# Rotation tables by doubling on ScalarE and VectorE, weight stores one half later, norm transposes later

## The chip, the cores and the metric

The kernel runs on one core of a Trainium2 chip. The metric is the device time of one execution in microseconds (us), and the time of the kernel before is the median of three runs. A core has five engines, each with a queue of its own that it works through in order: TensorE (PE, matmuls and transposes, results in PSUM), VectorE (DVE), ScalarE (ACT), GpSimd (POOL) and SyncE (SP, which here only issues DMAs). ACT and POOL issue DMAs too. Engines wait for one another by semaphores; a wait stands in the queue, and what is behind it waits as well.

## What is computed

One layer of a decoder trunk on x of 2048 x 1024 float32, with 256 memory tokens:

```python
h = rmsnorm(x, mix_norm_w);  proj = h @ w_in                       # 2816 + 12 columns
y_s5  = s5_mixer(proj[..., :256], ...)                             # 16 groups of a diagonal SSM, 64 complex states each
y_ssd = ssd_mixer(z, xbc, dt, ...)                                 # conv, chunks of 128, 12 heads
x = x + concat([y_s5, y_ssd]) @ w_out
x = x + cross_attention(rmsnorm(x), rmsnorm(mem), wq, wk, wv, wo)
x = x + conv_ffn(rmsnorm(x), w_up, conv_w, conv_b, w_down)
return rmsnorm(x, final_norm_w)
```

The part that the change touches most is the S5 group. Its recurrence over blocks of 8 steps is done as a real scan of magnitudes after a rotation, and for that each of the 16 groups needs a table of cos and sin, powers j = 0 to 255 of one unit complex number per state: 128 partitions x 2 x 256 values.

## The kernel before

The program is written with generators, and a framework turns it into one instruction order per engine, with semaphores where data or buffers demand them. The order on each engine follows the order of the text, with priorities and the framework's own forecast of what is ready when.

*Mixer (first 730 us).* `MixerIn.run` goes through four blocks of 512 rows (b = 0 to 3). Each block makes 22 projections (`proj`, n = 0 to 21): 24 matmuls of 128x512 each, since every float32 product is split into a high and a low fp32r part and done as three matmuls (`mm3`, L127 to L129). After each half projection `k.step()` advances three lists of generators by one `yield`: `fg` (the chunk scan `ssd` of the half block before), `bg` (`norm1_rest`, and `ssq` once per block) and `xg` (`s5_setup`, from the second half of block 0 on). So "one step later" means half a projection later.

*Weights.* `fetch` runs three projections ahead. A weight that is new is loaded into two staging tiles (tag `r`, L115), split on ACT (L102) and DVE (L103) into four tiles (tag `w`), and at one of the passes the split parts are stored to DRAM (`wSd`, L319); later blocks load the parts straight into `w` tiles (L317). `store` says at which block n is stored; up to and including that block it is loaded and split anew.

*Normed rows.* `norm1_rest` takes tiles t = 4 to 15 of 128 rows: load x, square on ACT (L140), mean on DVE (L134), power on POOL (L135), scale on DVE (L143), wait some steps, transpose on PE (L152), copy on ACT (L283), store to `h1T`. The next block's h is loaded from `h1T` (`fetch_h`) and split with gains on ACT and DVE (L105, L106) into tiles of tag `h`.

*Chunk scan.* `ssd` needs for each chunk the decay matrix L. `fetch_L` loads it by a broadcast DMA on POOL's queue (L406) into one of four slots, masks it with an affine select on POOL (L407), and ACT takes the exponential (L422) one chunk ahead. DVE multiplies it into M (L453), after which the slot is free. The convolutions (`conv`) run ACT L327, L330, three DVE steps L332, the tanh on ACT L334, DVE L335.

*Tables.* At its end `s5_setup` builds two tables of 16 entries, B (powers 0 to 15) and A (powers 16 a), by six small POOL products per doubling (L774 to L779), and then for every group g the outer product of the two: four products and two sums of 128x256 on POOL (L790 to L798), in three steps, and a DMA to `tabd` on POOL's queue (L799). `k.behind()` places those products in POOL's queue behind the last affine select of `fetch_L` (`k.mark`). `Er`, `Ei` hold the unit number raised to 2^q. `stage_s5` loads the tables back later.

After the mixer come the memory projections with `stage_s5`, attention, and the feed-forward part, which the change does not touch.

Of the kernel before, what the change touches and what calls it, by code (L numbers as in the profile page):

```python
# [9 lines left out]
F32 = mybir.dt.float32  # L10
F32R = mybir.dt.float32r
I32 = mybir.dt.int32
AF = mybir.ActivationFunctionType
ALU = mybir.AluOpType
AX = mybir.AxisListType
P = 128
# [8 lines left out]
def bcol(a, n):  # L25

    return a.rearrange("p (a b) -> p a b", b=1).to_broadcast([a.shape[0], a.shape[1], n])


class Kit:  # L30


    def __init__(self, tc, cx):
        self.tc, self.nc = tc, tc.nc
        self.V, self.S, self.G, self.TE = tc.nc.vector, tc.nc.scalar, tc.nc.gpsimd, tc.nc.tensor
        ep = cx.enter_context
        self.cp = ep(tc.tile_pool(name="const", bufs=1))
        self.dp = ep(tc.tile_pool(name="dram", bufs=1, space=bass.MemoryType.DRAM))
        self.pp = ep(tc.tile_pool(name="ps", bufs=8, space=bass.MemoryType.PSUM))
        self.sm = ep(tc.tile_pool(name="small", bufs=4))  # L40
        self.fg, self.bg, self.xg, self.mark = [], [], [], None
        nc = self.nc
        self.ident = self.cp.tile([P, P], F32, name="ident")
        make_identity(nc, self.ident)
        self.m05 = self.cp.tile([P, 1], F32, name="m05")
        nc.vector.memset(self.m05, -0.5)
        self.gains = self.cp.tile([P, 32], F32, name="gains")
# [38 lines left out]
    def drain(self, bg=False):  # L86
        for lst in (self.bg, self.xg) if bg else (self.fg,):
            while lst:
                try:
                    next(lst[0])  # L90
                except StopIteration:
                    lst.pop(0)

    def behind(self):

        return self.tc.issue_after(self.mark.ins)


    def halves(self, src, hi, lo, scale=None):
# [78 lines left out]
class MixerIn:  # L178
# [96 lines left out]
    def norm1_rest(self):  # L275
        k = self.k
        for t in range(4, self.T // 128):
            xs = self.norm1(t)
            for _ in range(3):
                yield  # L280
            ht = k.raw()
            for hf in range(2):
                k.S.activation(ht[:, hf * 512:hf * 512 + 512], k.tr4(xs, hf), AF.Copy)  # L283
                yield
            b, o = divmod(t * 128, 512)
            k.nc.scalar.dma_start(out=self.d["h1T"][b].rearrange("p (a n) -> p a n", a=8)[:, :, o:o + 128], in_=ht.rearrange("p (a n) -> p a n", a=8))
# [16 lines left out]
    def fetch(self):  # L303

        if not self.order:
            return
        k, (b, n, i) = self.k, self.order.pop(0)
        store = n // 11
        if b <= store:
            w = k.load2(self.a["w_in"][i])  # L310
        else:
            w = [[k.t(F32R, tag="w") for _ in range(2)] for _ in range(2)]
        for h in range(2):
            for q in range(2):
                s = self.d["wS"][i][:, 2 * h + q, :]
                if b > store:
                    k.nc.sync.dma_start(out=w[h][q].bitcast(F32), in_=s)  # L317
                elif b == store:
                    k.nc.sync.dma_start(out=s, in_=w[h][q].bitcast(F32))  # L319
        self.ahead.append(w)  # L320
# [81 lines left out]
    def fetch_L(self, b, pr, c):  # L402

        L = self.Ls[:, self.nL % 4]
        self.nL += 1
        self.k.G.dma_start(out=L.rearrange("p h l -> p (h l)"), in_=flat(self.d["acs"][b, c:c + 1, pr * 6:pr * 6 + 6, :]).partition_broadcast(P))  # L406
        self.k.mark = self.k.G.affine_select(out=L, in_=L, pattern=[[0, 6], [1, P]], compare_op=ALU.is_ge, fill=-1e30, base=0, channel_multiplier=-1)  # L407
        self.L[b, pr, c] = L

    def ssd(self, b, pr, dd, xs, Bs, Cs, zs, sqacc):  # L410
# [114 lines left out]

    def ssq(self, b, sqacc):
        k = self.k
        yield
        yield
        pq = k.ps()  # L530
        for c in range(4):
            k.TE.matmul(pq[:, c:c + 1], sqacc[:, c * 128:c * 128 + 128], self.one, start=True, stop=True)
        k.rstd(self.d["rs"][:, b * 4:b * 4 + 4], pq[:, 0:4], 0.25 / 768, 1e-6)
        yield
# [42 lines left out]
def s5_setup(k, a, d, up, NJ):  # L577

    nc, V, G, TE, S = k.nc, k.V, k.G, k.TE, k.S
    sp = d["s5p"]  # L580
# [57 lines left out]
    nst = NJ.bit_length() - 1  # L638
    Er, Ei = (sp.tile([P, nst + 3, 16], F32, tag=n, name=n) for n in ("Er", "Ei"))
    V.tensor_copy(Er[:, 0, :], cs)  # L640
    V.tensor_copy(Ei[:, 0, :], sn)
    for q in range(nst + 2):
        e, f = Er[:, q, :], Ei[:, q, :]
# [47 lines left out]
    b1, b2, Ca, Cb, Ba, Bb = (big(n) for n in ("b1", "b2", "Ca", "Cb", "Ba", "Bb"))  # L691
# [29 lines left out]
    for q in range(4):  # L721
# [26 lines left out]
        for w in range(2):  # L748
# [11 lines left out]
            put(d["ww"][gs, :, w * 128:w * 128 + 128], Ws)  # L760
            yield

    tw = sp.tile([P, 16, 8], F32, tag="tw", name="tw")
    few = []
    for n, q0 in (("B", 3), ("A", 7)):
        fc, fs = (sp.tile([P, 16, 16], F32, tag="5" + x, name="f" + x) for x in (("b1", "b2") if n == "B" else ("Ca", "Cb")))
        with k.behind():
            G.memset(fc[:, :, 0:1], 1.0)
            G.memset(fs[:, :, 0:1], 0.0)
        for q in range(4 if n == "B" else nst - 4):  # L770
            m = 1 << q
            er, ei, t = bcol(Er[:, q0 + q, :], m), bcol(Ei[:, q0 + q, :], m), tw[:, :, 0:m]
            co, so, ci, si = fc[:, :, m:2 * m], fs[:, :, m:2 * m], fc[:, :, 0:m], fs[:, :, 0:m]
            G.tensor_tensor(co, ci, er, op=ALU.mult)  # L774
            G.tensor_tensor(t, si, ei, op=ALU.mult)
            G.tensor_tensor(co, co, t, op=ALU.subtract)
            G.tensor_tensor(so, ci, ei, op=ALU.mult)
            G.tensor_tensor(t, si, er, op=ALU.mult)
            G.tensor_tensor(so, so, t, op=ALU.add)  # L779
            yield  # L780
        few.append((fc, fs))
    (cb, sb), (ca, sa) = few
    na = NJ // 16
    for g in range(16):
        tab = sp.tile([P, 2, na, 16], F32, tag="tab", name="tab", bufs=2)
        wk = sp.tile([P, 16, 16], F32, tag="5Ba", name="wk")[:, 0:na]
        a_ = lambda v: v[:, g, 0:na].rearrange("p (a b) -> p a b", b=1).to_broadcast([P, na, 16])
        b_ = lambda v: v[:, g, :].rearrange("p (a b) -> p a b", a=1).to_broadcast([P, na, 16])
        with k.behind():
            G.tensor_tensor(tab[:, 0], a_(ca), b_(cb), op=ALU.mult)  # L790
            G.tensor_tensor(wk, a_(sa), b_(sb), op=ALU.mult)
        G.tensor_tensor(tab[:, 0], tab[:, 0], wk, op=ALU.subtract)
        yield
        yield
        with k.behind():
            G.tensor_tensor(tab[:, 1], a_(sa), b_(cb), op=ALU.mult)
        G.tensor_tensor(wk, a_(ca), b_(sb), op=ALU.mult)
        G.tensor_tensor(tab[:, 1], tab[:, 1], wk, op=ALU.add)  # L798
        G.dma_start(out=d["tab"][g], in_=tab.rearrange("p h a b -> p h (a b)"))  # L799
        yield  # L800

def stage_s5(k, a, d, T):
# [748 lines left out]
def trunk(tc, a, out, T):  # L1553
    with ExitStack() as cx:
        k = Kit(tc, cx)
        nc = k.nc
        D = lambda shape, nm: k.dp.tile(shape, F32, name=nm)
        NJ = T // 8
        d = dict(h1T=D([T // 512, P, 4096], "h1T"), wS=D([22, P, 4, 512], "wSd"), G=D([8, P, 1024], "Gd"), VW=D([8, P, 1024], "VWd"), u=D([2, P, T], "ud"),
                 yT=D([T // 128, P, 8, 128], "yTd"), x1=D([T, 1024], "x1d"), x2=D([T, 1024], "x2d"), h3C=D([T // 1024, 7, 4, P, 512], "h3Cd"),  # L1560
                 tab=D([16, P, 2, NJ], "tabd"), ww=D([16, P, 256], "wwd"), cct=D([16, P, 384], "cctd"), Gt=D([4, 4, P, 512], "Gtd"), VWt=D([4, 4, P, 512], "VWtd"), p=D([T, 1024], "pd"), acs=D([T // 512, 4, 12, P], "acsd"), act=D([T // 128, P, 22, 128], "actd"),
                 rs=k.cp.tile([P, T // 128], F32, name="rs"), r8=k.cp.tile([P, 16], F32, name="r8"))
        with ExitStack() as c1:
            k.open(c1, 3, r=4, w=12, h=16, t=25)
            mem = Memory(k, a, d)
            with ExitStack() as c2:
                d["s5p"] = c2.enter_context(tc.tile_pool(name="s5p", bufs=1))
                mix = MixerIn(k, c2, a, d, T)
                mix.run(mem.prep(), s5_setup(k, a, d, mix.u, NJ))
                k.drain(bg=True)  # L1570
                K, Vt = mem.proj("wk", "wv"), mem.proj("wv", None)
                k.drain()
                k.drain(bg=True)
            k.fg.append(stage_s5(k, a, d, T))
            mem.scores(K, 2)
            mem.values(Vt, 2)
            after = k.at
            k.drain()
        with ExitStack() as c1:
            stage_b(k, c1, a, d, T, after)  # L1580
        with ExitStack() as c1:
            stage_up(k, c1, a, d, T)
        with ExitStack() as c1:
            stage_down(k, c1, a, d, out, T)
# [40 lines left out]
```

## Time and profile before

| | |
|---|---|
| median of three runs | 2728.22 us (2726.66 to 2729.36) |
| profiled execution | 2734.65 us, its span 2732.9 us |
| PE busy | 2635.3 us (96% of the span) |
| DVE, ACT, POOL busy | 2070.4, 1263.3, 488.6 us |
| mean granted PE clock | 0.987 |
| DMA | 520.14 MB, 190 GB/s mean |

The profile is one execution with every instruction's start and duration. Lines of the timeline give the start, the length, the engine, the line of the kernel, the operation, what is written and read, and in brackets how long the engine stood idle before it and which instruction released it. A matmul of 128x512 shows 0.39 us, but they overlap: one starts every 0.23 us. Where PE's granted clock falls below 1 the same matmuls start further apart, and this counts as busy time. The rows of the page's groups give the sum, the mean and the idle time before.

### The profile page before, as it was taken

How to read it: one execution, taken by the hardware profiler on the slowest of the kernel's cores; microseconds unless marked ns; L12 is line 12 of the kernel's file. 1: busy time of each engine (PE TensorE's matmuls, PEld its weight loads, DVE VectorE, ACT ScalarE, POOL GpSimd, SP SyncE). 2: the span in 40 equal slices, each digit the busy share in tenths (PEclk: the TensorE clock that was granted, in tenths of full speed). 3: DMA queues.
4: the chain of work that ended last, by engine and by line, in shares of the span. 5: the costliest groups of instructions: out<-in, count | busy, mean ns of one | idle time of the engine just before them, and what ended most of it. 6: DMA issues, size and time to landing. Idle time of an engine off the chain costs nothing. (4 is left out here: it accounts for less than half of the span.)

```text
span 2732.9 us, 38473 instructions
## 1 busy us (share of the span) xinstructions
PE 2635.3 (96%) x12636; PEld 2192.9 (80%) x12636; DVE 2070.4 (76%) x3809; ACT 1263.3 (46%) x2547; POOL 488.6 (18%) x807
## 2 busy tenths in 40 slices
PE   7889999989999999999999999999999999999998
PEld 6778878768888788887887888887888887878876
DVE  5887887676866655778789788889888787677776
ACT  4553543225444413687745455445434344433333
POOL 0111145622013110110311222212111110000000
PEclk9999999989999999999999999999999999999999
DMA  9666866557478774537665333425232227887886
GB/s 297 204 198 214 286 207 209 174 163 215 126 234 274 278 260 162 179 138 239 220 218 172 112 116 120 139 82 181 85 92 77 87 62 258 279 286 240 261 265 204
DMA packets 270048, 520.14 MB, mean 190 GB/s; under 512 B 33176, under 2 KB 75224, under 8 KB 269848
## 3 DMA queue, kind: packets, MB, share of 16 engines
q1 hardware_dynamic: 210824, 393.30, 44.2%
q0 software_dynamic: 30416, 105.50, 12.0%
q10 hardware_dynamic: 28608, 18.88, 2.2%
q8 instruction: 100, 1.64, 0.2%
q14 instruction: 100, 0.82, 0.1%
HBM read 379.51 MB, written 137.46 MB: 189 GB/s over the span
## 5 line engine op out<-in xcount | busy, mean ns | idle before, releaser
L128 PE MATMUL ps<-H,W 128*128 128x512 f32 x952 | 370.8, 390 | 0.5 <-DVE H L103 0.5
L127 PE MATMUL ps<-H,W 128*128 128x512 f32 x952 | 370.9, 390 | 0.4 <-ACT H L102 0.4
L129 PE MATMUL ps<-H,W 128*128 128x512 f32 x952 | 370.5, 389 | 0.0
L127 PE MATMUL ps<-h,w 128*128 128x512 f32 (+1 forms) x736 | 300.9, 409 | 10.7 <-ACT h L105 8.1
L128 PE MATMUL ps<-h,w 128*128 128x512 f32 (+1 forms) x736 | 289.4, 393 | 4.4 <-DVE h L106 4.3
L129 PE MATMUL ps<-h,w 128*128 128x512 f32 (+1 forms) x736 | 288.6, 392 | 0.2 <-DVE w L103 0.2
L127 PE MATMUL ps<-Q,A 128*128 128x512 f32 x704 | 275.8, 392 | 2.0 <-ACT M L1052 1.2
L129 PE MATMUL ps<-Q,A 128*128 128x512 f32 x704 | 274.4, 390 | 0.0
L128 PE MATMUL ps<-Q,A 128*128 128x512 f32 x704 | 273.9, 389 | 0.0
L102 ACT ACTIVATE W<-S 128x512 fp32r<-128x512 f32 x191 | 118.9, 630 | 284.2 <-DVE S L1379 145.4
L128 PEld LDWEIGHTS ps<-H,W 128*128 128x128 f32 x952 | 178.7, 188 | 38.9 <-DVE H L103 2.1
L127 PEld LDWEIGHTS ps<-H,W 128*128 128x128 f32 x952 | 178.7, 188 | 37.9 <-ACT H L102 0.8
L129 PEld LDWEIGHTS ps<-H,W 128*128 128x128 f32 x952 | 178.7, 188 | 37.1 <-DVE W L103 0.2
L127 PEld LDWEIGHTS ps<-h,w 128*128 128x128 f32 x736 | 141.3, 192 | 37.2 <-ACT h L105 8.8
L128 PEld LDWEIGHTS ps<-h,w 128*128 128x128 f32 x736 | 141.0, 192 | 33.7 <-DVE h L106 9.5
L129 PEld LDWEIGHTS ps<-h,w 128*128 128x128 f32 x736 | 140.9, 191 | 29.3 <-DVE w L103 0.4
L127 PEld LDWEIGHTS ps<-Q,A 128*128 128x128 f32 x704 | 132.2, 188 | 29.1 <-ACT M L1052 1.5
L129 PEld LDWEIGHTS ps<-Q,A 128*128 128x128 f32 x704 | 132.1, 188 | 28.6 <-DVE A L103 1.1
L128 PEld LDWEIGHTS ps<-Q,A 128*128 128x128 f32 x704 | 132.2, 188 | 26.9
L102 ACT ACTIVATE A<-F 128x512 fp32r<-128x512 f32 (+1 forms) x146 | 89.1, 631 | 124.0 <-PE ps L128 75.7
L332 DVE SCALAR_TENSOR_TENSOR t<-t,cw 128x512 f32<-128x512 f32 x168 | 139.4, 830 | 7.7 <-ACT t L330 5.8
L103 DVE TENSOR_TENSOR W<-S,W 128x512 fp32r<-128x512 f32 x191 | 130.3, 685 | 7.1 <-ACT W L102 5.4
(489 smaller groups left out, 6180.9 us busy)
## 6 DMA issues: line engine op xcount, KB each, us to landing
w<-wSd SPq DMA_DIRECT2D x220, 256.0 KB, 3.9
A<-actd SPq DMA_DIRECT2D x192, 256.0 KB, 3.9
R<-in_w_up SPq DMA_DIRECT2D x176, 256.0 KB, 3.1
R<-in_w_down SPq DMA_DIRECT2D x132, 256.0 KB, 4.3
wSd<-w SPq DMA_DIRECT2D x88, 256.0 KB, 3.7
actd<-U POOLq DMA_DIRECT2D x88, 256.0 KB, 3.1
A<-actd SPq DMA_DIRECT2D x96, 192.0 KB, 3.7
r<-in_w_in SPq DMA_DIRECT2D x66, 256.0 KB, 4.5
```

The source lines that it names most:

```text
L102: self.S.activation(hi, src, AF.Copy)
L103: self.V.tensor_tensor(lo, src, hi.bitcast(F32), op=ALU.subtract)
L127: self.TE.matmul(out, lh, rh, start=first and i == 0, stop=False)
L128: self.TE.matmul(out, lh, rl, start=False, stop=False)
L129: self.TE.matmul(out, ll, rh, start=False, stop=last and i == n - 1)
L332: k.V.scalar_tensor_tensor(xc, gb[:, q:q + 512], cw[:, j, q:q + 1], xc, op0=ALU.mult, op1=ALU.add)
```

## The change

The outer product of two short tables on POOL is replaced, for every group, by doubling on ACT and DVE: the first 16 entries are copied from B, then at q = 4 to 7 ACT makes two scaled copies of the first 2^q entries and one DVE scalar_tensor_tensor makes the next 2^q of both halves. B itself moves to DVE. `behind` and `mark` go. The steps from the first table on are 4 + 16 x 3 in place of 8 + 16 x 3. Further: n < 11 are stored at block 1 and n >= 11 at block 0 (before: the other way round); `norm1_rest` waits five steps in place of three, `ssq` five in place of two; and the tile pools have `r=6, w=10` in place of `r=4, w=12`.

```diff
 norm1_rest:
             xs = self.norm1(t)
-            for _ in range(3):
+            for _ in range(5):
                 yield
 fetch:
-        store = n // 11
+        store = int(n < 11)
 fetch_L:
-        self.k.mark = self.k.G.affine_select(out=L, ...)
+        self.k.G.affine_select(out=L, ...)
 ssq:
-        yield
-        yield
+        for _ in range(5):
+            yield
 s5_setup:
+    En = sp.tile([P, nst + 3, 16], F32, tag="En", name="En")
+    V.tensor_scalar(En, Ei, -1.0, None, op0=ALU.mult)
     tw = sp.tile([P, 16, 8], F32, tag="tw", name="tw")
-    (A and B by six G.tensor_tensor per doubling, memsets behind the mark)
+    fc, fs = (sp.tile([P, 16, 16], F32, tag="5" + x, name="f" + x) for x in ("b1", "b2"))
+    V.memset(fc[:, :, 0:1], 1.0)
+    V.memset(fs[:, :, 0:1], 0.0)
+    for q in range(4):
+        m = 1 << q
+        er, ei, t = bcol(Er[:, 3 + q, :], m), bcol(Ei[:, 3 + q, :], m), tw[:, :, 0:m]
+        co, so, ci, si = fc[:, :, m:2 * m], fs[:, :, m:2 * m], fc[:, :, 0:m], fs[:, :, 0:m]
+        for x, u, v, op in ((co, ci, si, ALU.subtract), (so, si, ci, ALU.add)):
+            V.tensor_tensor(x, u, er, op=ALU.mult)
+            V.tensor_tensor(t, v, ei, op=ALU.mult)
+            V.tensor_tensor(x, x, t, op=op)
+        yield
     for g in range(16):
-        (six G.tensor_tensor of 128x256, three yields, the DMA)
+        tab = sp.tile([P, 2, NJ], F32, tag="tab", name="tab", bufs=2)
+        w = sp.tile([P, 2, NJ // 2], F32, tag="5Ba", name="w")
+        S.activation(tab[:, 0, 0:16], fc[:, g, :], AF.Copy)
+        S.activation(tab[:, 1, 0:16], fs[:, g, :], AF.Copy)
+        for q in range(4, nst):
+            m, e = 1 << q, 3 + q
+            S.activation(w[:, 0, 0:m], tab[:, 1, 0:m], AF.Copy, scale=En[:, e, g:g + 1])
+            S.activation(w[:, 1, 0:m], tab[:, 0, 0:m], AF.Copy, scale=Ei[:, e, g:g + 1])
+            V.scalar_tensor_tensor(tab[:, :, m:2 * m], tab[:, :, 0:m], Er[:, e, g:g + 1], w[:, :, 0:m], op0=ALU.mult, op1=ALU.add)
+            if q % 2:
+                yield
+        G.dma_start(out=d["tab"][g], in_=tab)
+        yield
 trunk:
-            k.open(c1, 3, r=4, w=12, h=16, t=25)
+            k.open(c1, 3, r=6, w=10, h=16, t=25)
```

More of the change, by code (lines that the diff above doesn't have):

```diff
@@ L40, in __init__ @@
         self.sm = ep(tc.tile_pool(name="small", bufs=4))
-        self.fg, self.bg, self.xg, self.mark = [], [], [], None
+        self.fg, self.bg, self.xg = [], [], []
         nc = self.nc
@@ L92, in drain @@
                     lst.pop(0)
-    def behind(self):
-        return self.tc.issue_after(self.mark.ins)
     def halves(self, src, hi, lo, scale=None):
@@ L406, in fetch_L @@
         self.k.G.dma_start(out=L.rearrange("p h l -> p (h l)"), in_=flat(self.d["acs"][b, c:c + 1, pr * 6:pr * 6 + 6, :]).partition_broadcast(P))
-        self.k.mark = self.k.G.affine_select(out=L, in_=L, pattern=[[0, 6], [1, P]], compare_op=ALU.is_ge, fill=-1e30, base=0, channel_multiplier=-1)
+        self.k.G.affine_select(out=L, in_=L, pattern=[[0, 6], [1, P]], compare_op=ALU.is_ge, fill=-1e30, base=0, channel_multiplier=-1)
         self.L[b, pr, c] = L
@@ L761, in s5_setup @@
             yield
+    En = sp.tile([P, nst + 3, 16], F32, tag="En", name="En")
+    V.tensor_scalar(En, Ei, -1.0, None, op0=ALU.mult)
     tw = sp.tile([P, 16, 8], F32, tag="tw", name="tw")
[L764 to L781, printed above, removed]
@@ L782, in s5_setup @@
-    (cb, sb), (ca, sa) = few
-    na = NJ // 16
-    for g in range(16):
[L785 to L799, printed above, removed]
+    fc, fs = (sp.tile([P, 16, 16], F32, tag="5" + x, name="f" + x) for x in ("b1", "b2"))
```

## The prediction

> **What bounds the kernel now.** I read the page first, then the order of TensorE (PE) in the timeline for its gaps, then busy time by stage, then the chain behind the largest gap.
>
> ```profile
> span 2732.9 us, 38473 instructions
> PE 2635.3 (96%) x12636; PEld 2192.9 (80%) x12636; DVE 2070.4 (76%) x3809; ACT 1263.3 (46%) x2547; POOL 488.6 (18%) x807
> ```
>
> PE is busy for 2635.3 of 2732.9 us and the change leaves its work alone, so only PE's 97.6 us of idle time and the stretches at a lower granted clock can be won. The change acts on the mixer, roughly the first 730 us. Columns of the next view: the stage, its length, then busy us of PE, weight loads, DVE, ACT and POOL, the granted clock, the DMA share, GB/s.
>
> ```profile
> 20.00:60.00 40.00, 36.43 (x166) 27.57 (x166) 20.19 (x76) 15.16 (x28) 1.10 (x2) 0.96 0.92 290
> 60.00:120.00 60.00, 51.02 (x236) 41.36 (x234) 44.48 (x145) 37.74 (x81) 8.60 (x13) 0.97 0.74 241
> 120.00:200.00 80.00, 70.62 (x369) 60.10 (x368) 68.90 (x215) 40.63 (x86) 11.40 (x15) 0.94 0.58 181
> 200.00:300.00 100.00, 99.82 (x542) 82.59 (x540) 77.81 (x178) 46.81 (x98) 19.87 (x26) 1.00 0.79 249
> 300.00:340.00 40.00, 38.89 (x213) 33.64 (x214) 31.52 (x60) 17.55 (x38) 5.51 (x7) 1.00 0.79 257
> 340.00:400.00 60.00, 54.55 (x267) 42.87 (x267) 47.75 (x91) 27.61 (x53) 28.96 (x61) 0.91 0.69 216
> 460.00:540.00 80.00, 75.47 (x386) 63.62 (x385) 55.84 (x86) 20.93 (x46) 52.49 (x69) 1.00 0.62 187
> 540.00:580.00 40.00, 29.53 (x114) 20.13 (x113) 31.56 (x43) 18.62 (x34) 22.98 (x29) 0.74 0.61 190
> 580.00:680.00 100.00, 100.00 (x522) 85.34 (x520) 66.53 (x153) 36.11 (x87) 18.66 (x24) 1.00 0.62 186
> 440.00:640.00 200.00, 185.00 (x912) 151.97 (x911) 143.30 (x252) 72.51 (x160) 105.78 (x135) 0.95 0.65 197
> ```
>
> The last row overlaps others and serves further down. I take as lost in a stage: idle time plus busy time x (1 - clock). That gives 5.0 us (20 to 60), 10.5 (60 to 120), 13.6 (120 to 200), 0.2, 1.1, 10.4 (340 to 400), 4.5 (460 to 540), 18.1 (540 to 580), 0: 63.4 us in all, the most that this change can win. The gaps behind it, in PE's timeline (idle before, and releaser, in brackets):
>
> ```profile
> 24.45 5.42 PE L353 MATMUL ps<-h,wd 128*24 128x512 f32 x16 [3.57 <-DVE ear L166]
> 169.38 1.54 PE L476 MATMUL ps<-u 128*128 128x64 f32 x6 [4.20 <-DVE u L453]
> 379.94 0.50 PE L127 MATMUL ps<-h,w 128*128 128x512 f32 x1 [1.76 <-ACT h L105]
> 551.22 0.79 PE L127 MATMUL ps<-h,w 128*128 128x512 f32 x1 [6.37 <-ACT h L105]
> 729.07 0.33 PE L440 MATMUL ps<-ident,t 128*128 128x128 f32 x1 [1.55 <-DVE t L335]
> ```
>
> and one group from who PE waits for (total us, times, longest):
>
> ```profile
> PE ps L152 <- DVE raw L143: 10.3, 3, 4.7
> ```
>
> The largest, 6.37 us at 551, is a queue of waits that begins on POOL:
>
> ```profile
> 533.82 0.62 POOL L797 TENSOR_TENSOR wk<-fCa,fb 128x256 f32<-128x256 f32 x1
> 534.38 0.59 POOL L406 DMA_DIRECT2D L<-acsd  x1
> 540.13 0.86 POOL L407 TENSOR_SCALAR_AFFINE_SELECT L<-L 128x768 f32<-128x768 f32 x1 [5.16 <-DMA L<-acsd]
> 541.02 1.87 ACT L422 ACTIVATE L<-L,nacs 128x128 f32<-128x128 f32 x6 [12.92 <-POOL L L407]
> 543.44 0.69 DVE L335 SCALAR_TENSOR_TENSOR t<-t 128x512 f32<-128x512 f32 x1 [9.51 <-ACT t L334]
> 702.78 0.55 POOL L406 DMA_DIRECT2D L<-acsd  x1 [9.02 <-DVE u L453]
> 709.11 1.87 ACT L422 ACTIVATE L<-L,nacs 128x128 f32<-128x128 f32 x6 [4.33 <-POOL L L407]
> ```
>
> The decay DMA (L406) goes out on POOL's queue only after the table products there (L790 to L798); ACT stands at L422 for 12.92 us, its next tanh (L334) waits behind it, DVE stands 9.51 us for that tanh, and the splits of the next block's h wait behind both. In the last block, with the products done, the same step starts when its slot is free: ACT stands 4.33 us, and PE, at 729, only 1.55. That is the control for the first part. All waits of this kind at 380 to 551 (total, times, longest):
>
> ```profile
> ACT L L422 <- POOL L L407: 33.9, 6, 12.9
> ```
>
> **(a) Tables off GpSimd: -14 us, and +5 for their new place.** Removed are six products for each of 16 groups and 48 small ones:
>
> ```profile
> L798 POOL TENSOR_TENSOR tab<-tab,wk 128x256 f32<-128x256 f32 x16 | 14.9, 934 | 0.9
> L790 POOL TENSOR_TENSOR tab<-fCa,fb 128x256 f32<-128x256 f32 x16 | 12.5, 780 | 0.2
> L332 DVE SCALAR_TENSOR_TENSOR t<-t,cw 128x512 f32<-128x512 f32 x28 | 29.6, 1056 | 0.6
> L332 DVE SCALAR_TENSOR_TENSOR t<-t,cw 128x512 f32<-128x512 f32 x29 | 22.2, 765 | 3.1 <-ACT t L330 2.6
> L326 DVE COPY t<-halo 128x3 f32<-128x3 f32 x9 | 4.7, 527 | 0.0
> L326 DVE COPY t<-halo 128x3 f32<-128x3 f32 x10 | 1.6, 160 | 0.0
> ```
>
> The two ends of six such groups, about 13.5 us each, make some 80 us of POOL that no longer stand ahead of L406. The DVE pairs are first the stretch 446 to 540, with products, then 645 to 730, without: the same L332 takes 1056 against 765 ns, the copy 527 against 160. So DVE gets back 28 x 0.29 = 8.1 us and 9 x 0.37 = 3.3 us, and about as much for the other halo copy (an estimate): 15 us per 94 us, some 30 over the 200 us of tables.
>
> Added to DVE: 24 products of 128x16 to 128x128, and per group four scalar_tensor_tensor of 2 x 16, 32, 64, 128 elements. Added to ACT: per group two copies of 128x16 and eight scaled copies of 128x16 to 128x128. Nearest rows:
>
> ```profile
> L644 DVE TENSOR_TENSOR t<-Er,Ei 128x16 f32<-128x16 f32 x10 | 1.7, 169 | 0.0
> L170 DVE SCALAR_TENSOR_TENSOR e1p<-e1p,e1r 128x16 f32<-128x16 f32 x5 | 0.9, 171 | 0.1
> L395 ACT ACTIVATE E<-acs 128x48 f32<-128x48 f32 x3 | 0.7, 246 | 3.9 <-DVE acs L385 3.9
> L422 ACT ACTIVATE L<-L,nacs 128x128 f32<-128x128 f32 x173 | 56.4, 393 | 85.0 <-POOL L L407 71.6 <-DVE t L326 5.7 <-DVE t L646 5.6
> ```
>
> Between 171 ns (16 elements) and 765 (512) lie 1.2 ns per element: 0.19 + 0.23 + 0.30 + 0.45 = 1.2 us per group, 19 for 16 groups, and 24 x 0.23 = 6 us of products: 25 us on DVE against the 30 it gets back. ACT: eight of about 0.24 and two of 0.39, 2.7 us per group, 43 us, where ACT is busy for 20.93 of 80 us; hidden as busy time. What is not hidden is the order: each of 64 DVE steps waits for two ACT copies and the next copies for it, in queues that run in order, with L422's waits ahead on ACT and L332 and L335 behind on DVE. No row shows such a pair under this load; the bounds are 0 (each hides in a gap of 3.5 us between steps) and some 25 us (rival 1). I take 5, near the lower end, since DVE has 24 of 80 us free at 460 to 540 and ACT 59.
>
> Of the 22.6 us lost at 460 to 580 I leave 8.5: the next block's boundary then looks like that of 380, whose share of the 340 to 400 loss is about that, gap and clock together. Gain 14 (bounds 0 and 21).
>
> [...]
>
> **(b) Stores of the first eleven weights go to the second block's pass: -3, and +2.** In block 0 n < 11 were stored at once; now n >= 11 are, and n < 11 are loaded and split a second time in block 1. The count stays 88 stores and 22 second splits. SP's own queue:
>
> ```profile
> 12.55 3.77 SPq L319 DMA_DIRECT2D wSd<-w  x7
> 18.27 0.43 SPq L218 DMA_DIRECT2D al<-in_ssd_alog  x1
> ```
>
> Seven stores went ahead of the small loads on which L166 (the 3.57 us gap at 24) waits, and the DMAs were 92% busy at 290 GB/s at 20 to 60. I take 3 of the 5.0 lost there (bounds 0 and 5). The stores now stand in SP's queue at 80 to 190, where the share is 0.58 to 0.74; each waits for its split, and the loads behind it wait too, but those loads need the same split's slots. What a split costs DVE:
>
> ```profile
> L103 DVE TENSOR_TENSOR w<-r,w x114: 672/684/1149, 11.8 to 855.2; 128x512 fp32r<-128x512 f32 x114
> ```
>
> Eleven weights x 2 x 0.684 us = 15 us of DVE move from the second half of block 1 to its first; DVE has 22 us free at 200 to 300, but little at 180 to 200: +2 (bounds -1, since 300 to 340 is relieved, and 8).
>
> **(c) Norm transposes two steps later, sums of squares three: -8.** The three waits on L143 (10.3 us, all before 200) are PE reaching the transposes before the scaled rows exist; two more steps are two half projections, over 5 us of other PE work. The x loads, the square on ACT, POOL's power and the store of each tile move later with them: 12 tiles need 84 steps in place of 60, and each block's h is read after 28, 56 and 84, which its steps still cover (44 and one per block). But DVE is the bound nearby, 68.90 of 80 us, so part of what PE does not wait here it waits later (the 4.20 at 169 stays). From 60 to 200 lose 24.1: I take 5 before 120 and 3 after (bounds 0 and 14). The sums of squares held no PE: 0.
>
> **(d) Six staging tiles for loads, ten for split weights: -2, and +1.** Two more of the next block's h rows can be fetched before the old ones are split, which shortens the 1.76 us at 380 and what its clock costs (bounds -5 and +2). Weights have 10 tiles in place of 12: one half projection less of lead, still four halves, about 11 us, against a landing of 3.9 (median):
>
> ```profile
> w<-wSd SPq DMA_DIRECT2D x220, 256.0 KB, 3.9
> ```
>
> +1 (bounds 0 and 5).
>
> **Sum.** -14 + 5 - 3 + 2 - 8 - 2 + 1 = -19 us. The profiled execution took 2734.65 us (1.75 outside its span), 6.4 above the median 2728.22 of the three runs; I carry the difference to the median: 2709.
>
> **Rivals.**
> 1. *The table chain holds the conv chain (slower).* At an L422 wait ACT now has table copies in its queue, and a DVE step that waits for them stands ahead of L332 and L335. Blocks 2 and 3 have some ten such waits, six of them with 33.9 us. DVE is busy 143 of 200 us at 440 to 640 and so has 57 to give; ten waits of 4 to 5 us take 45 of them, and I put half on PE, 24 us, with the boundary gap left as it is (no -14, and the 5 is in the 24): -19 + 14 - 5 + 24 = +14, 2742. It makes the kernel slower from about 16 us of PE time. Against it: the steps come one per half projection, and ACT is half idle.
> 2. *The waits only change their name (no change).* L406 waits for L453 in most blocks (9.02 us at 702), so a free POOL may find no free slot; and with DVE at 86% at 120 to 200, PE falls behind it anyway. Then (a) gives 5, (c) 1, (b) 1, the costs eat them: 2727.
> 3. *Nearly all goes.* Without contention on DVE, 540 to 580 keeps only the 1.55 us kind of gap and 60 to 200 loses half: -38, 2690.
>
> **How the numbers follow.** Forecast 0.50, its own range 2697 to 2722; rival 1 0.21, rival 2 0.19, rival 3 0.10. The range 2690 to 2736 goes from the third rival to inside the first and leaves out some 2 in 10. 0.2% (5.5 us) is what a measurement of this kernel tells from no change: faster is the forecast and rival 3, with a little of rival 2 falling on that side, 0.61; same 0.18; slower 0.21.
>
> **What the next profile would show.** (a) no TENSOR_TENSOR of tables on POOL, L332 near 765 ns in the third block, ACT's wait at L422 near 4 us throughout, PE's gap at the third boundary under 2 us; new waits of DVE on the table copies below 1 us each. (b) no store on SP before 60 us, the gap at 24 shorter. (c) no wait of L152 on L143. (d) h splits that wait less for their loads. Wrong would make it: DVE standing for table copies in the tens of us, a new gap at the first boundary (h loads and split loads share six tiles), or PE waiting for w.

## The result, and the profile after

The kernel after takes 2695.62 us (median of four runs, 2685.60 to 2696.07), beside 2727.68 for the kernel before (2726.66 to 2729.36, likewise four): ratio 0.9873, 95% interval 0.985 to 0.9897, so some 34 us faster (here and below a ratio is one of means, and the times are medians). The profiled execution took 2695.32 us, near its median; that of before lies 7 us above its own, so differences between these two traces (39.3 us of span) read a few us too large.

Line numbers of the kernel after are four lower from `halves` to `ssd` (the matmuls L123 to L125, the splits of h L101 and L102, the conv steps L328, the decay DMA L402, its mask L403, the exponential L418). The table copies are L777 to L782, the DVE step L783, the table DMA L786. The head of the page after:

```profile
span 2693.6 us, 38616 instructions
PE 2621.5 (97%) x12636; PEld 2183.4 (81%) x12636; DVE 2052.8 (76%) x3900; ACT 1301.5 (48%) x2707; POOL 389.4 (14%) x659
```

POOL lost 99 us of busy time; ACT gained 38, and DVE is 18 us lower although it took over the table work. The busy times by stage, columns as in the prediction:

```profile
20.00:60.00 40.00, 40.00 (x188) 31.60 (x187) 37.34 (x255) 16.32 (x30) 1.87 (x3) 1.00 0.41 132
60.00:120.00 60.00, 56.44 (x269) 47.04 (x268) 38.91 (x75) 36.90 (x82) 8.70 (x13) 0.97 0.79 268
120.00:200.00 80.00, 73.17 (x360) 57.68 (x359) 65.06 (x147) 42.05 (x83) 10.31 (x13) 0.94 0.79 258
200.00:300.00 100.00, 95.47 (x516) 80.15 (x515) 79.71 (x188) 47.84 (x102) 20.77 (x25) 0.98 0.81 262
300.00:340.00 40.00, 40.00 (x228) 35.09 (x227) 26.90 (x55) 15.44 (x37) 7.34 (x10) 1.00 0.67 211
340.00:400.00 60.00, 54.84 (x299) 44.08 (x298) 45.63 (x112) 31.29 (x68) 7.11 (x10) 1.00 0.77 238
460.00:540.00 80.00, 74.04 (x366) 62.03 (x365) 55.19 (x126) 48.90 (x147) 11.14 (x17) 0.96 0.62 187
540.00:580.00 40.00, 38.81 (x205) 31.01 (x205) 27.37 (x75) 9.23 (x17) 0.00 (x0) 1.00 0.58 190
```

By the prediction's measure (idle time plus busy time x (1 - clock)) the losses are 0, 5.3, 11.2, 6.4, 0, 5.2, 8.9 and 1.2: 38 us where it was 63.4. The stage that won most is the one with the largest gap before, 540 to 580 (18.1 to 1.2). Then come 60 to 120, 340 to 400 and 20 to 60 with some 5 us each; in the last of them the DMAs are 41% busy in place of 92%. Two stages lose more than before: 200 to 300 (0.2 to 6.4) and 460 to 540 (4.5 to 8.9). In PE's timeline the gaps over 2 us between 20 and 700 us, and what is left at the third boundary, are now these:

```profile
99.42 0.33 PE L436 MATMUL ps<-ident,t 128*128 128x128 f32 x1 [3.56 <-DVE t L331]
267.18 1.11 PE L753 MATMUL ps<-ident,t 128*128 128x128 f32 x4 [3.00 <-DVE t L712]
377.38 0.44 PE L436 MATMUL ps<-ident,t 128*128 128x128 f32 x2 [2.69 <-DVE t L331]
465.03 0.48 PE L436 MATMUL ps<-ident,t 128*128 128x128 f32 x1 [2.46 <-DMA w<-wSd]
542.73 0.50 PE L124 MATMUL ps<-h,w 128*128 128x512 f32 x1 [0.46 <-DVE h L102]
```

The 3.57 us at 24 are gone, no wait on the scaled rows is left, and of the 6.37 us at the third boundary 0.46 stay. The chain that made that gap began on POOL; its decay DMA now, and the step of DVE that frees its slot:

```profile
519.35 0.55 DVE L449 TENSOR_TENSOR u<-L,ps 128x384 f32<-128x384 f32 x1
520.45 0.55 POOL L402 DMA_DIRECT2D L<-acsd  x1 [4.43 <-issue]
```

The DMA goes out 0.55 us after that step has ended. Before, the same step and the DMA (at 534.38, shown above) stood like this:

```profile
525.01 0.54 DVE L453 TENSOR_TENSOR u<-L,ps 128x384 f32<-128x384 f32 x1
```

It ended at 525.55, and the DMA went out 8.8 us later; POOL worked through table products and their stores nearly all of that time. So the late decay DMA was POOL's doing, as the prediction read it.

ACT's waits now, at 380 to 560 (total, times, longest):

```profile
ACT L L418 <- POOL L L403: 13.1, 6, 3.6
```

Six waits as before, 13.1 us in place of 33.9, the longest 3.6 in place of 12.9. What came in its place, the waits between 380 and 640:

```profile
DVE tab L783 <- ACT w L782: 22.9, 21, 3.7
ACT w L781 <- DVE tab L783: 18.3, 32, 1.2
ACT tab L777 <- DMA tabd<-tab: 17.2, 10, 3.2
```

and the groups of the new instructions (busy us, mean ns of one, idle time before them):

```profile
L783 DVE SCALAR_TENSOR_TENSOR tab<-tab,Er,w 128x256 f32<-128x256 f32 x16 | 7.7, 483 | 8.7 <-ACT w L782 8.5
L781 ACT ACTIVATE w<-tab,En 128x128 f32<-128x128 f32 x16 | 6.4, 400 | 6.8 <-DVE tab L783 6.7
L781 ACT ACTIVATE w<-tab,En 128x16 f32<-128x16 f32 x16 | 4.9, 304 | 3.5 <-DVE tab L783 3.4
```

DVE stands 22.9 us for table copies, in 21 waits, and ACT 18.3 for the DVE steps. PE stands for a table instruction itself only once (0.4 us, at 204), but the waits reach it through the queues. Ahead of PE's gap at 465:

```profile
461.85 0.22 ACT L777 ACTIVATE tab<-fb 128x16 f32<-128x16 f32 x1 [3.17 <-DMA tabd<-tab]
462.58 0.35 DVE L783 SCALAR_TENSOR_TENSOR tab<-tab,Er,w 128x128 f32<-128x128 f32 x1 [2.68 <-ACT w L782]
464.29 0.69 DVE L331 SCALAR_TENSOR_TENSOR t<-t 128x512 f32<-128x512 f32 x1
```

ACT's first copy of a table (L777) waits for the store of the table two groups before. The scaled copies stand behind it in ACT's queue, DVE's L783 waits for them, and the last conv step and L331 stand behind that. L331 ends at 464.98, and PE's transpose L436 starts at 465.03. The profile puts the wait of that transpose down to a load of `w`, but its row reads `ident` and `t`, no weight; `t` is what L331 wrote. DVE's steps from 446 to 540 are at the pace that the prediction took from the last block:

```profile
L328 DVE SCALAR_TENSOR_TENSOR t<-t,cw 128x512 f32<-128x512 f32 x27 | 20.2, 747 | 3.4 <-ACT t L326 3.3
L322 DVE COPY t<-halo 128x3 f32<-128x3 f32 x9 | 1.5, 163 | 0.0
```

1056 ns became 747, 527 became 163. The trace of before shows the same without a second kernel: of its conv steps between 380 and 720 us, the 42 that run beside neither a product nor an affine select of POOL take 748 ns on average, and the 37 that overlap a table product 1048.

The stage that the prediction did not look at is the memory projections with S5, before (722 to 910) and after (700 to 877), each from its first product to the first attention product. Before, the busy times and ACT's waits for loads:

```profile
722.00:910.00 188.00, 172.34 (x1203) 158.95 (x1202) 132.84 (x248) 97.88 (x221) 30.28 (x68) 0.97 0.66 219
```

```profile
ACT w L102 <- DMA r<-in_wo: 10.2, 6, 3.0
ACT w L102 <- DMA r<-in_wqT: 7.9, 4, 3.5
ACT w L102 <- DMA r<-in_wv: 7.4, 5, 2.4
```

After:

```profile
700.00:877.00 177.00, 167.70 (x1202) 156.16 (x1201) 131.21 (x244) 96.72 (x218) 30.46 (x68) 0.99 0.67 228
```

```profile
ACT w L98 <- DMA r<-in_wqT: 5.1, 2, 4.0
ACT t L98 <- DMA r<-in_wqT: 2.9, 1, 2.9
ACT w L98 <- DMA r<-in_wv: 0.2, 1, 0.2
```

The same work takes 11 us less (7 in a second profiled execution, below). Its weights come through the same staging tiles (tag `r`), of which there are now six: ACT's split stands 8.2 us for loads in place of 25.5. The description above calls the part behind the mixer untouched. Its instructions are, but these buffers are not.

### The profile page after: what moved, and what is told of

Its sections match the earlier page's. It is cut to its first block, busy times and chain, and to the rows that moved or that the text cites. A ratio compares the mean times of both kernels' runs of the same rounds, so it can differ in the third digit from the quotient of the medians.

```text
span 2693.6 us, 38616 instructions
## 1 busy us (share of the span) xinstructions
PE 2621.5 (97%) x12636; PEld 2183.4 (81%) x12636; DVE 2052.8 (76%) x3900; ACT 1301.5 (48%) x2707; POOL 389.4 (14%) x659
## 5 line engine op out<-in xcount | busy, mean ns | idle before, releaser
L123 PE MATMUL ps<-H,W 128*128 128x512 f32 x952 | 371.3, 390 | 0.0
L125 PE MATMUL ps<-H,W 128*128 128x512 f32 x952 | 371.0, 390 | 0.0
L123 PE MATMUL ps<-h,w 128*128 128x512 f32 (+1 forms) x736 | 301.8, 410 | 5.5 <-DVE h L102 2.0
L125 PE MATMUL ps<-h,w 128*128 128x512 f32 (+1 forms) x736 | 288.6, 392 | 0.0
L123 PE MATMUL ps<-Q,A 128*128 128x512 f32 x704 | 276.2, 392 | 0.8 <-ACT A L98 0.8
L125 PE MATMUL ps<-Q,A 128*128 128x512 f32 x704 | 274.8, 390 | 0.0
L125 PEld LDWEIGHTS ps<-H,W 128*128 128x128 f32 x952 | 178.7, 188 | 37.4 <-DVE W L99 0.4
L123 PEld LDWEIGHTS ps<-H,W 128*128 128x128 f32 x952 | 178.7, 188 | 37.4 <-ACT H L98 0.4
L123 PEld LDWEIGHTS ps<-h,w 128*128 128x128 f32 x736 | 141.1, 192 | 33.4 <-ACT h L101 3.1
L125 PEld LDWEIGHTS ps<-h,w 128*128 128x128 f32 x736 | 140.6, 191 | 29.6
L125 PEld LDWEIGHTS ps<-Q,A 128*128 128x128 f32 x704 | 132.2, 188 | 28.4 <-DVE A L99 1.1
L123 PEld LDWEIGHTS ps<-Q,A 128*128 128x128 f32 x704 | 132.2, 188 | 28.0 <-ACT A L98 1.0
L328 DVE SCALAR_TENSOR_TENSOR t<-t,cw 128x512 f32<-128x512 f32 x168 | 127.3, 758 | 17.6 <-ACT t L326 15.8
```

Source lines behind the costliest of these rows:

```text
L123: self.TE.matmul(out, lh, rh, start=first and i == 0, stop=False)
L125: self.TE.matmul(out, ll, rh, start=False, stop=last and i == n - 1)
L328: k.V.scalar_tensor_tensor(xc, gb[:, q:q + 512], cw[:, j, q:q + 1], xc, op0=ALU.mult, op1=ALU.add)
```

## The experiments

Theory: the time went with POOL's products (the third boundary, DVE's pace), with SP's early stores (the start), and with the staging tiles (wherever a load was waited for). Rivals: one part carries all of it and the others only rename waits; or the steps "later" carry block 0, as the prediction had it. First the four parts, each alone on the kernel before.

**Tables alone.** `s5_setup` as in the change, all else as before.

> The kernel before with the tables alone moved to ACT and DVE. Theory 1 (the gain of the tables is the third boundary, where POOL's products stood ahead of the decay DMA): 10 to 14 us faster, the gap of 6.4 us at 551 gone, block 0 unchanged. Theory 2 (the gain is DVE time that no longer contends with POOL, spread over blocks 1 to 3): 5 to 8 us, spread. Theory 3 (the handoffs ACT to DVE eat it): 0 to 4 us faster or slower.

**Stores alone.** The first eleven weights are stored one block later, the last eleven one block earlier.

```diff
-        store = n // 11
+        store = int(n < 11)
```

> The kernel before with the two halves of the weight stores exchanged alone. Theory 1 (SP's queue and DMA load at the start): the wait at 24 us (3.57 us) and its clock go, 3 to 5 us faster. Theory 2 (the splits moved into the first half of block 1 and the stores into the DVE-bound half of block 0 cost as much): within 2 us of before.

**Later alone.** `norm1_rest` five steps in place of three, `ssq` five in place of two.

> The kernel before with the norm transposes and the sums of squares later alone. Theory 1: the three waits of PE on L143 (10.3 us) go, 5 to 9 us faster by the end of block 0. Theory 2 (DVE is the bound in block 0, so PE waits elsewhere for the same time): within 3 us of before.

**Pools alone.** `r=6, w=10` in place of `r=4, w=12`.

> The kernel before with six staging tiles and ten weight tiles alone. Theory 1 (as predicted, only the boundaries): 0 to 3 us faster. Theory 2 (the 11 us that the changed kernel gained between the start of block 3 and the attention stage come from the staging tiles in the memory products): 8 to 11 us faster, all after 570 us.

Then the other way round: the whole change with one of the four parts undone.

> The changed kernel with its tables back on POOL. Alone the tables gave 5 us, stores 6, pools 10, the later steps nothing: 19 to 20, where the whole gave 34. Theory A (the parts need each other: the table move pays once the loads no longer hold the boundaries): about 2710, that is 14 to 18 us above the changed kernel. Theory B (the other three need each other, not the tables): 5 us above it.

> The changed kernel with the stores of the weights as before. Theory A (stores free block 0, so that the later steps have something to give): 10 to 14 us above the changed kernel, all of it by the end of block 0. Theory B (independent): 6 us above it.

> The changed kernel with the norm transposes and sums of squares at their old steps. Theory A (with the stores moved, PE in block 0 runs ahead and waits for the scaled rows again): 5 to 9 us above the changed kernel, by the end of block 0. Theory B (as alone: nothing): within 2 us of it.

> The changed kernel with r=4, w=12. Theory A (the staging tiles pay in the memory products, whatever else is changed): 9 to 11 us above the changed kernel, after 570 us. Theory B (they pay mainly at the boundaries with the tables' ACT work beside): more than 12 us, at the boundaries.

And the whole again, beside the variants further down:

> The changed kernel once more, beside the three below, for a narrower interval: the parts left out one at a time cost 8.5, 7.6, 3 and 11 us, 30 together, so 28 to 35 us faster than before.

Measured, each as a ratio to the kernel before run beside it, with its 95% interval; the whole gave 0.9874 (0.9851 to 0.9897) when measured again, 2699.48 us beside 2731.86. The last columns are us at 2731, the median of before in these runs; undoing is counted against that 0.9874:

| part | alone | whole without it | us alone | us lost by undoing it |
|---|---|---|---|---|
| tables | 0.9981 (0.9967 to 0.9995) | 0.9904 (0.9889 to 0.992) | -5 | 8 |
| stores | 0.9979 (0.9968 to 0.999) | 0.9901 (0.988 to 0.9921) | -6 | 7 |
| later | 1.0005 (0.9993 to 1.0016) | 0.9884 (0.9865 to 0.9904) | +1 | 3 |
| pools | 0.9965 (0.9954 to 0.9975) | 0.9914 (0.9899 to 0.9929) | -10 | 11 |

Alone they come to -20 us, together to -34. A figure of the first us column is uncertain by 3 to 4 us, one of the second by some 8, since two intervals enter it. So the pools are worth something both ways, the tables too, though by undoing only just; the stores are worth something alone, and their 7 is not clear of noise. No part carries it all; the pools are worth most; "later" by itself is worth nothing that can be measured, and in the whole 3 us, within its interval.

Beside what was expected: "later" alone came out as its second theory had it, and the stores alone a little above their first. The tables alone gave 5 where theory 1 had 10 to 14, although the gap that it named went; the gain was not spread over blocks 1 to 3 either, as theory 2 had it. The pools alone gave the 10 of theory 2, but not all after 570 us. Undoing the tables (8) and "later" (3) fell between their theories, undoing the stores (7) near theory B, undoing the pools (11) on theory A by its size, and the whole again (34) in its range.

To see where, I read from each trace when ACT takes the result of each block's first projection (L552 before, L548 after), and when the first memory product and the first attention product start. A block runs to that point in the next, so the slow start of a block counts for the one before it; block 0 runs from the start of the span. The table has the change of each stage's length against before, in us. These are single executions, each a few us off its median: the last column, the same work after the mixer and S5 in all of them, shows the scatter, and so do the two executions of the whole.

| kernel | block 0 | block 1 | block 2 | block 3 | memory and S5 | rest |
|---|---|---|---|---|---|---|
| whole | -8.7 | -1.5 | -11.8 | -0.4 | -10.8 | -6.1 |
| whole, again | -11.7 | -1.7 | -9.5 | -0.4 | -7.2 | -4.7 |
| tables | +1.9 | -1.2 | -8.0 | -0.3 | -4.2 | -1.2 |
| stores | -2.5 | +0.5 | -0.9 | +0.1 | -0.9 | -5.8 |
| later | -4.1 | +6.6 | -1.0 | -0.3 | +4.0 | -4.5 |
| pools | -9.0 | +5.1 | -2.1 | +0.8 | -9.4 | +0.7 |

*Tables* act in block 2. The third boundary with the tables alone, and DVE's waits for table copies (380 to 640):

```profile
460.00:540.00 80.00, 73.65 (x350) 61.85 (x350) 53.55 (x124) 47.25 (x154) 10.92 (x17) 0.91 0.60 181
540.00:580.00 40.00, 38.01 (x185) 29.13 (x184) 26.84 (x65) 17.14 (x29) 0.57 (x1) 1.00 0.71 216
```

```profile
DVE tab L783 <- ACT w L782: 23.4, 20, 4.5
```

540 to 580 loses 2.0 us in place of 18.1, but 460 to 540 now 13.0 in place of 4.5, PE waiting there for DVE. One of its gaps there, 2.88 us at 475.55, has the same path behind it as the gap at 465 above: at 472 to 473 ACT stands 3.44 us for a table store, and DVE 2.94 us for ACT's copies. With everything but the tables, the longest wait at L422 is nearly the old one (380 to 560), the conv steps keep most of their old slowness (440 to 535), and the gap at the third boundary is back:

```profile
ACT L L422 <- POOL L L407: 25.7, 5, 11.4
```

```profile
L332 DVE SCALAR_TENSOR_TENSOR t<-t,cw 128x512 f32<-128x512 f32 x25 | 24.6, 983 | 0.9 <-ACT t L330 0.4
```

```profile
534.94 0.49 PE L127 MATMUL ps<-h,w 128*128 128x512 f32 x1 [4.51 <-ACT h L105]
```

Block 2 lasts 175.8 us in place of 168.3 (170.6 in the second execution of the whole): 5 to 7.5, where the tables alone give 8.0.

*Stores* act at the start. With the stores alone 20 to 60 loses 0.9 us in place of 5.0 (the DMAs 50% busy), but PE's wait at the transposes at the end of block 0, 3.61 us before, grows. The busy times, the wait, and the same wait, longer still, in the whole without "later":

```profile
20.00:60.00 40.00, 39.09 (x184) 30.65 (x183) 37.01 (x252) 18.27 (x34) 2.34 (x4) 1.00 0.50 158
```

```profile
191.65 1.09 PE L152 MATMUL ps<-ident,raw 128*128 128x128 f32 x4 [8.45 <-DVE halo L328]
```

```profile
193.31 1.09 PE L148 MATMUL ps<-ident,raw 128*128 128x128 f32 x4 [13.02 <-DVE halo L324]
```

The profile names the halo copies, but the scaled rows that these transposes read were ready only just before: DVE ended the scaling (L143, then L139) at 191.50 and 193.17. In the whole, with the transposes two steps later, neither wait is there. So "later" has a use, but one that the stores' move makes. The 13 us of this gap are not what it is worth, since undoing "later" costs 3 us. Where the whole loses by the old order of the stores its single trace doesn't show: a gap at the start is back (5.05 us at 27), yet block 0 takes no more time than in the whole (197.1 us beside 201.6 and 198.6).

*Later.* The waits on L143 before 200 us nearly go, as forecast (10.3 to 0.7 us), and come back elsewhere. Two gaps of this kernel, and the busy times of the stretch before the first:

```profile
111.03 0.48 PE L440 MATMUL ps<-ident,t 128*128 128x128 f32 x1 [8.50 <-DVE t L335]
371.52 0.90 PE L152 MATMUL ps<-ident,raw 128*128 128x128 f32 x3 [6.85 <-DVE raw L143]
```

```profile
95.00:111.00 16.00, 7.53 (x36) 6.03 (x34) 15.48 (x76) 11.70 (x25) 0.59 (x1) 0.82 0.46 148
```

DVE is busy for 15.48 of the 16 us: it works through conv steps, weight splits and the 16-element steps of `s5_setup`, and PE waits for it, at the transposes or elsewhere. And the twelve tiles now reach further into block 1 (84 steps in place of 60, at 44 a block), whose end gets the wait that block 0 lost.

*Pools* act where loads are waited for: 60 to 120 loses 4.1 us in place of 10.5, and from 200 to 620 ACT no longer stands for the next block's h rows (8.4 us in 5 waits before, none with the pools alone, 0.2 in the whole). The busy times of 60 to 120 with the pools alone:

```profile
60.00:120.00 60.00, 55.86 (x266) 45.77 (x265) 47.77 (x138) 38.22 (x83) 9.20 (x14) 1.00 0.76 254
```

ACT's waits for loads in the memory stage (702 to 886) of the whole without the pools:

```profile
ACT w L98 <- DMA r<-in_wv: 8.7, 5, 3.0
ACT w L98 <- DMA r<-in_wo: 8.1, 6, 3.7
ACT w L98 <- DMA r<-in_wqT: 7.6, 6, 2.3
```

Every kernel with six staging tiles passes that stage in 177 to 181 us, every one with four in 183 to 191; ACT's waits on these loads come to 7 to 12 us with six tiles and to 24 to 27 with four, in all fourteen traces. The gap at the third boundary stays with the pools alone (5.22 us at 545) and goes with the tables: that one is POOL's.

**Three variants of the whole.** Ten weight tiles in place of twelve were expected to cost something. Twelve fit beside six staging tiles when `t` gives up one:

```diff
-            k.open(c1, 3, r=6, w=10, h=16, t=25)
+            k.open(c1, 3, r=6, w=12, h=16, t=24)
```

> The changed kernel with twelve weight tiles again (r=6, w=12, and t=24 in place of 25 to make room). Theory A (ten tiles cost something: PE's 2.46 us gap at 465 that ends on a load of w): 2 to 5 us faster than the changed kernel, that gap gone. Theory B (four halves of lead are enough, the gap is chance): within 2 us.

Ratio 0.9859 (0.9834 to 0.9884), 2694.45 us: not to be told from the whole. No wait of PE is put down to a load of `w` in this trace, as theory A had it, but the time is no shorter; PE now waits here, on the same path from the table copies as above:

```profile
466.73 0.80 PE L445 MATMUL ps<-t 128*128 128x128 f32 x2 [4.83 <-DVE t L331]
```

So the gap at 465 was not for want of weight tiles.

**A third table buffer.** `bufs=3` for `tab`, so that the first copies need not wait for the DMA two groups back (ACT stands 17.2 us there).

> The changed kernel with three table tiles in place of two: ACT's first copy of a group no longer waits for the store of the table two groups before (17 us in 10 waits at 380 to 560). Theory A (that wait is part of the 23 us that DVE stands for table copies, and so of the 9 us that PE loses at 460 to 540): 2 to 5 us faster than the changed kernel. Theory B (it only moves the wait within the chain): within 2 us.

Ratio 0.9868 (0.9844 to 0.9892), 2696.42 us: no difference either. But the wait that it was meant to take away stayed:

```profile
ACT tab L777 <- DMA tabd<-tab: 16.6, 10, 3.0
```

ACT's first copies now stand one group earlier in its queue and wait for the same stores, three groups back. So the run doesn't show what that wait is worth; with the gap at 465 hanging on it, it stays a candidate for more.

**POOL's queue filled with something else.** Was it the occupied queue, or that the products take from DVE? Eight small DMAs per group, 128 in all, behind the affine select as the products were:

```diff
+    def fill(g, i, n):
+        with k.tc.issue_after(k.mark.ins):
+            for j in range(i, i + n):
+                G.dma_start(out=d["fil"][g * 8 + j], in_=k.ident[0:16, 0:16])
```

> The changed kernel with POOL's queue filled again: 128 tiny DMAs from a constant tile, eight per group of about 0.6 us each, stand behind the affine selects where the products stood (their data are not used; the result of the kernel is the same). They hold POOL's queue as the products did but touch no operand tile of DVE. Theory A (what the products cost was their place ahead of the decay DMA): the wait of ACT at the decay exponentials rises to 6 us and more, the third boundary's gap comes back, 6 to 9 us above the changed kernel. Theory B (what they cost was DVE's slower steps): within 2 us of the changed kernel, L332's successor at 750 ns.

Ratio 0.9876 (0.985 to 0.9902), 2699.36 us: nothing. Its POOL rows, ACT's waits at 380 to 560, and DVE's conv steps at 446 to 530:

```profile
508.72 11.46 POOL L777 DMA_DIRECT2D fild<-ident  x24
520.52 0.59 POOL L402 DMA_DIRECT2D L<-acsd  x1 [0.34 <-issue]
```

```profile
ACT L L418 <- POOL L L403: 16.7, 6, 5.2
```

```profile
L328 DVE SCALAR_TENSOR_TENSOR t<-t,cw 128x512 f32<-128x512 f32 x23 | 18.3, 797 | 1.6 <-ACT t L326 1.4
```

POOL was occupied for 11.46 us before the decay DMA, but that DMA went out at 520.5 as in the whole, since its slot came free only then (DVE's L449 ended at 519.98). ACT's longest wait, 5.2 us, stayed under the 6 of theory A, and no gap came back at the boundary. DVE kept its pace: the conv steps at 517.64 and 518.77, which run wholly beside those issues, take 0.74 and 0.75 us. The mean of 797 has steps beside affine selects in it: two from 523.88, with an affine select from 524.46, take 2.01 us together, where two from 508.96 take 1.53. So the fillers' queue time cost nothing where it delayed nothing. It is no test of a decay DMA made late. In the kernel before that DMA was 8.8 us late and DVE's steps were slower as well; how the cost of the products divides between the two stays open.

## Why the prediction was right, and where its terms were off

It forecast 2709 us, from 2690 to 2736; 2695.62 is inside, 13 us below, and between the forecast and rival 3 (2690). Its reading of the third boundary and of the start was right. Two of its four terms were not: (c) gave nothing and (d) was far too small, and that the sum fits is in part luck. Term by term, alone and undone beside the forecast:

- **(a) Tables, -14 + 5 = -9.** Measured -5 alone, 8 lost by undoing, 5 to 8 in block 2. The steps held: no products on POOL, L328 at 747 ns, ACT's longest wait 3.6, 0.46 us at the third boundary. The durations held too: 1.40 us per group on DVE (forecast 1.2). The handoffs were mis-described: waits "below 1 us each" were forecast, 1.1 us on average and up to 3.7 came, 22.9 us in all, which the prediction itself had named as a sign of being wrong. Rival 1 needed ten waits of 4 to 5 us on DVE with the boundary gap left; neither is there. But its path is: ACT's table copies hold DVE's conv steps, and these hold PE. That is what stands behind the gap at 465, and 460 to 540 went from 4.5 us lost to 8.9 (13.0 with the tables alone). The +5 is thus about right for the whole and too low for the tables alone, as far as this stage measures it; not every gap in it was traced.
- **(b) Stores, -3 + 2 = -1.** Measured -6 alone (-9 to -3), 7 undone (not clear of noise). The gain at the start was 4.1 to 5 us, the upper bound. The price was foreseen in its place, before 200 us: a gap of 8.45 us alone, where 3.61 stood before, and none in the whole.
- **(c) Later, -8.** This step failed: +1 alone (-2 to +4), 3 undone (not clear of noise). The prediction read the 10.3 us of waits on L143 as time to be won, although it noted in the same place that DVE is the bound there. With DVE busy 97% of the stretch, taking this wait away only showed the next one.
- **(d) Pools, -2 + 1 = -1.** Measured -10 alone (-13 to -7), 11 undone: the term most mis-sized. The forecast looked for staging tiles only at the block boundaries; they pay in block 0 and as much in the memory stage behind the mixer, 9.4 us alone and 4 to 7 undone (183.8 us in place of 176.5 and 180.2, the two executions of the whole). That stage lies outside the 63.4 us that the prediction took for the most to be won. The +1 for ten weight tiles was not there: twelve measure the same.
- **The sum.** Alone, the four give -20, close to the -19 forecast, by luck: (c) was 9 too good and (d) 9 too poor, (a) 4 too good and (b) 5 too poor. The other 14 us, uncertain by some 9, are what the parts do for one another. Seen of this is one piece: the gap of 8.45 to 13.0 us at 190, which the moved stores make and "later" takes away. Block 1 got longer with "later" alone and with the pools alone (+6.6, +5.1) and not in the whole. The products that still run on POOL in those two do not explain it by themselves: in the whole without the tables they run too, and block 1 takes 180.8 us, as before (181.0). Where the rest of the 14 us comes from stays open.

Rival 2, that waits only change their name, is what happened to (c), and in part to (a) at 460 to 540. On the clock, 540 to 580 went from 0.74 to 1.00 when 0.46 was left of the 6.37 us gap there, so the 7.7 us that the clock took (29.53 x 0.26) came back. In the kernel before, the granted clock was 0.50 from 551 to 568 (the 128x512 matmuls at 562.37 and 562.79 start 0.42 us apart), and gaps of 0.41 to 1.97 us broke PE's work up to 564. The two stages from 460 to 580, where (a) counted on 14 us, together lost 12.5 us less in the whole (22.6 to 10.1) and 7.6 less with the tables alone.

## What to carry to other kernels

A wait that you can name is won only if the engine behind it has time to spare (here DVE, busy for 15.48 of 16 us, had none, and "later" alone gave nothing): look at the busy share of the releasing engine in just that stretch, and if it is near 100%, move work off that engine, not the waiter. When a buffer count is changed, list every stage that draws on that pool, also the ones whose code the change does not touch, and look there for waits on its loads. Follow a wait past the name that the profile gives it: ask what the waiting instruction reads, and who wrote that last. And test parts both alone and undone from the whole: alone, the parts here fell 14 us short of the whole's 34.

## What the runs showed of the hardware

Beside POOL's products on SBUF tiles DVE's two-input conv steps took 1056 ns in place of 747 (983 in the second kernel that has the products), and 3-element copies 527 in place of 163. In the trace of before the conv steps that overlap a product take 1048 ns and those that overlap neither a product nor an affine select 748, while the step with one operand in PSUM (L453) takes 546 beside a product and 550 without. The price here was 0.30 us per overlapped 128x512 step. A string of DMA issues on POOL, 11.46 us long, did not slow the conv steps: two wholly beside it took 0.74 and 0.75 us. A scaled copy on ACT took 304 ns for 16 elements per partition and 400 for 128, so eight times the data cost a third more.
